# Seven products for both halves of the columns in seven K chunks, with their summed weights made in DRAM on a list of their own

## The chip, the cores and the metric

The kernel runs on one core of one Trainium2 chip. Such a core has a matrix engine (TensorE, in the profile PE, with its weight loads as PEld), a vector engine (VectorE, DVE), an engine for functions and copies (ScalarE, ACT), GpSimd (POOL) and SyncE (SP), each with an instruction queue that it works through in order. Matrix products read SBUF and write PSUM; 16 DMA engines move data between DRAM and SBUF, and within DRAM. SP, ACT and POOL issue DMAs from their queues. Engines wait for each other through semaphores.

The metric is the device time of one execution in microseconds. The kernel before takes 2182.21 us, the median of three runs (2182.13 to 2182.46).

## What is computed

Two layers work on x of 256 positions by 2048 features, in float32. Layer 0 has a mixer of pooling and attention, layer 1 an mLSTM mixer; each is followed by the same kind of feed-forward block, which this change is about:

```python
def conv_ffn(x, w_up, conv_w, conv_b, w_down):
    u = x @ w_up                                        # 2048 -> 2 * 5632
    up = jnp.pad(u, ((0, 0), (1, 1), (0, 0)))
    c = conv_w.astype(u.dtype)
    u = c[0] * up[:, :-2] + c[1] * up[:, 1:-1] + c[2] * up[:, 2:] + conv_b.astype(u.dtype)
    gate, val = jnp.split(u, 2, axis=-1)
    return (jax.nn.silu(gate) * val) @ w_down           # 5632 -> 2048
...
        x = x + conv_ffn(rms_norm(x, norm_ffn[layer]), w_up[layer], conv_w[layer], conv_b[layer], w_down[layer])
```

## The kernel before

**Numbers in two parts.** Each float32 operand is split into a high part (a rounded copy in the type float32r, made by ACT) and a low part (the rest, a subtraction on DVE). A product is then three products: high by high, high by low, low by high.

**Weights as a stream.** All weights come in one list of 128 x 1024 tiles (512 KB; some are half as wide), in the order in which TensorE needs them. `Stream` takes each through three steps: `load` (a DMA on SP into one of six raw buffers `w`), `split` (the ACT copy at L121 and the DVE subtraction at L122, into one of four buffers `hl`) and `next` (TensorE uses it). Loads are written out five tiles ahead of the use, splits two. Two kinds of entries are special. A `Sum` is loaded by `prepare` into a buffer `sum`: one DMA on SP, then a second one on POOL that adds onto it (L106, L107). A `Chain` is the tile behind a `Sum`: its own load on SP, and then two DVE additions of half a tile each (L117, L118), by which it becomes two further sums of weights. `Sum`s are prepared as soon as they stand within ten tiles of the use.

**The feed-forward block.** The 5632 inner features are worked on in six chunks of K, `FCH = [4, 8, 8, 8, 8, 8]` tiles of 128 features. An "up" unit (`up`, named `up` in the profile) computes one tile of 128 gate features and its 128 value features: 64 matmuls into one of two PSUM buffers `mm`, over four weight tiles. Behind it ACT and DVE gather the result, multiply it by the norm, do the convolution and the SiLU gate, and write the two parts of the inner activation `g`. Then chunk c's activation is multiplied by the down weights and added to x.

The down product of a chunk is done in two ways. The ordinary way (`down`, in the profile `dn`) multiplies by a block of 512 of the 2048 output columns. The other way is the scheme of seven products for a 2 by 2 block matrix product in the place of eight (a Strassen form with few additions): positions are halved (128 and 128), a pair of K tiles is the inner halves, and a half of the columns (1024) is the two blocks of 512. `combine` makes the sums of activations of one pair (`sf`, `s3`, `s1`), the host lays out sums of weights as far as two terms go, and `Sum` and `Chain` make the rest. Per pair there is an A step (four products, 12 matmuls, two weight tiles) and a B step (three products, 9 matmuls, one tile and a half one), named `pp` in the profile. Over the pairs of a chunk the products add up in PSUM (`ps`, four buffers), and at the last pair DVE adds them onto x and onto three running sums `acc` (`unit`). `total` adds the running sums to x, six additions, once all chunks are through.

Which half goes which way is said by `_halves`: in each of the first five chunks the second half (h = 1) goes by seven products and the first half by `down`; the last chunk is all ordinary (`down_two`, `down`, `down_end`). `BOTH`, chunks with seven products for both halves, is empty.

**What sets the order.** `_ffn_plan` writes the order of the block: chunk c's products are spread between the up units of chunk c + 1. Each up unit of a chunk of eight is followed by one step: A of pairs 0 to 3, then B of pairs 0 to 3; two of them also by an ordinary product. I call an up unit's followers a slot. TensorE's instructions run in exactly the written order. Those of the other engines are ordered by a list scheduler ahead of time, by its own timeline. Small tasks beside the main work (norms, attention heads, totals) are generators in `Weave`, which the code resumes at points of a clock of its own that each product advances (`tick`); an up unit counts 10.32 there, and four blocks of the output projection 82.6.

**Names and lines that the change touches.** `Stream.load` and `prepare` (L89 to L108), `Weave` (from L146), `mm` (L237), `combine` (L947), `unit` and `total` (from L968 and L1013), the loop over the plan (L1085), `_halves`, `_ffn_plan`, `_down_chunks`, `_ffn_weights` (from L1160). POOL's queue also holds the reciprocal square roots of all norms (L245); ACT's also the row copies for the mLSTM heads (L795).

Of the kernel before, what the change touches and what calls it, by code (L numbers as in the profile page):

```python
# [9 lines left out]
F32 = mybir.dt.float32  # L10
# [23 lines left out]
CH = 8  # L34
BOTH = ()
NEG = -1.0e30
# [34 lines left out]


class Chain:

# [5 lines left out]
class Stream:  # L80
# [8 lines left out]
    def load(self, pieces=1):  # L89
        i = self.n_load  # L90
        self.n_load += 1
        src = self.srcs[i]
        if isinstance(src, Sum):
            i in self.w or self.prepare(i)
            return
        src = src.src if isinstance(src, Chain) else src
        width = src.shape[-1]
        n = width // pieces
        w = self.wpool.tile([P, CH * P], F32, tag="w", name=f"w{i}")
        for c in range(0, width, n):  # L100
            self.nc.sync.dma_start(w[:, c : c + n], src[:, c : c + n])
        self.w[i] = w, n, width

    def prepare(self, i):
        w = self.sums.tile([P, CH * P], F32, tag="sum", name=f"sum{i}")
        self.nc.sync.dma_start(w, self.srcs[i].one)  # L106
        self.nc.gpsimd.dma_start(w, self.srcs[i].other, accum_op=ALU.add)  # L107
        self.w[i] = w, CH * P, CH * P  # L108
# [37 lines left out]
class Weave:  # L146


    def __init__(self):
        self.t, self.q = 0.0, []  # L150
# [40 lines left out]
@with_exitstack  # L191
def trunk(ctx: ExitStack, tc: tile.TileContext, gx, xT, xn, call, catt, cml, weights, out):
    nc = tc.nc
# [39 lines left out]
    def gain(n, k):  # L233
        c = n * KT + k
        return gcol[:, c : c + 1]

    def mm(out_, lhsT, rhs, start, stop):  # L237
        pe.matmul(out_, lhsT, rhs, start=start, stop=stop, skip_group_check=True)  # L238

# [462 lines left out]
    def mlstm_layer(norm, nxt):  # L702
        with ExitStack() as es:
# [203 lines left out]
    def ffn_layer(layer, norm, nxt):  # L907
        with ExitStack() as es:
# [59 lines left out]
            def unit(kind, c, h, j):  # L968
# [33 lines left out]
                else:  # L1002
# [4 lines left out]
                    if c == len(FCH) - 2:  # L1007
                        wv.add(total(h), 12.0 if h else 2.0)

# [74 lines left out]
            f, gts = 0, []  # L1084
            for kind, c, i, *j in _ffn_plan():  # L1085
                if kind == "up":
# [72 lines left out]

def _halves(c):  # L1160

    return () if c == len(FCH) - 1 else (0, 1) if c in BOTH else (1,)


def _ffn_plan():

# [5 lines left out]
    for c, n in enumerate(FCH):  # L1172
        pairs = FCH[c - 1] // 2 if c else 0
        units = [(kind, c - 1, h, j) for h in (_halves(c - 1) if c else ()) for kind in "AB" for j in range(pairs)]
        per = max(1, len(units) // n)

        busy = {u[3]: k // per for k, u in enumerate(units) if u[0] == "A"}
        for i in range(n):
            seq.append(("up", c, i))
            seq += units[i * per : i * per + per]  # L1180
            if len(_halves(c - 1)) == 1:
                for b in range(2):
                    if pairs and i == (b + 1) * pairs // 2 - 1:
                        seq.append(("down", c - 1, b))
# [5 lines left out]
def _down_chunks(w):  # L1190


    out, k0 = [], 0
    for c, n in enumerate(FCH):
        rows = w[k0 * P : (k0 + n) * P]
        blocks = [_mov(rows[:, b * 512 : b * 512 + 512]) for b in range(NB) if b // 2 not in _halves(c)]
        if c == len(FCH) - 1:
# [16 lines left out]

def _ffn_weights(up, parts):

    down = iter(parts[0])
    out, u = [], 0
    for kind, c, i, *j in _ffn_plan():
        if kind == "up":  # L1220
# [4 lines left out]
        elif kind != "mix":  # L1225
            s0, s1, r, ba, bb = parts[1 + 5 * i : 6 + 5 * i]
            q = sum(FCH[:c]) // 2 + j[0]
            out += [Sum(s0[q], s1[q]), Chain(r[q])] if kind == "A" else [ba[q], bb[q]]
    return out

# [99 lines left out]
```

## Time and profile before

| | |
|---|---|
| median of three runs | 2182.21 us |
| the profiled execution | 2182.76 us, of which the span of its instructions is 2181.0 us |
| granted TensorE clock | 1.0 |
| busy share: TensorE, DVE, ACT, POOL | 100%, 77%, 63%, 3% |
| weights and data moved by DMA | 462.95 MB |

In time, attention and its output projection end near 256 us; layer 0's feed-forward block runs to 980, the mLSTM mixer with its output projection to 1457, layer 1's feed-forward block to the end. The trace is read by groups (what a kind of instruction takes), by waits (who waited for whom), by the chain that ended last, by order of time, and by stretches (busy time of each engine between two points of time). Names are those of the program: `w` a raw weight tile, `hl` a split one, `xx` the normed x in two parts. A matmul's or a copy's duration includes its start and its end, which overlap with its neighbours; from start to start it is shorter.

### The profile page before, as it was taken

The numbers are of one execution on the slowest core, as the hardware profiler recorded it, in microseconds if no ns is written. First come the engines' busy times: TensorE is split into PE (matmuls) and PEld (weight loads), VectorE is DVE, ScalarE is ACT, GpSimd is POOL, SyncE is SP. The second block draws the span as 40 slices with busy tenths as digits, with TensorE's granted clock in tenths as the row PEclk, the third lists the DMA queues.
The fourth block names the chain that finished last, engine by engine and source line by source line (L and its number), as shares of the span: only waits on it lengthen the run. The fifth ranks groups of instructions, "written<-read, shape, count | busy, mean of one in ns | idle before, by whom it ended". The sixth has DMA issues, their size and how long they took to land.

```text
span 2181.0 us, 31219 instructions
## 1 busy us (share of the span) xinstructions
PE 2175.4 (100%) x11508; PEld 1862.8 (85%) x11508; DVE 1670.8 (77%) x2366; ACT 1370.6 (63%) x2166; POOL 59.3 (3%) x76
## 2 busy tenths in 40 slices
PE   9999999999999999999999999999999999999999
PEld 7888888888888888889888888888888888888887
DVE  7686688887878788776777676668888787878776
ACT  7665576766767576666454554557676666757663
POOL 0010000000000000000000000000000000000000
PEclk9999999999999999999999999999999999999999
DMA  9556567676877766656465555756768677776664
GB/s 326 178 169 203 174 199 235 206 244 206 256 226 245 229 221 215 219 193 205 160 201 182 180 179 175 223 182 197 232 205 243 214 240 236 242 230 227 215 213 163
DMA packets 133595, 462.95 MB, mean 212 GB/s; under 512 B 14810, under 2 KB 17154, under 8 KB 133442
## 3 DMA queue, kind: packets, MB, share of 16 engines
q1 hardware_dynamic: 125024, 438.08, 60.0%
q0 software_dynamic: 5344, 19.14, 5.2%
q10 hardware_dynamic: 3074, 3.75, 0.7%
q8 instruction: 90, 1.47, 0.3%
q14 instruction: 63, 0.52, 0.1%
HBM read 458.76 MB, written 2.14 MB: 211 GB/s over the span
## 4 chain that ended last, share of the span: by engine, by line
PE 99%; DMA 1%; DVE 0%; ACT 0%; issue 0%; SPq 0%; DVEq 0%
PE up L238 44%; PE dn L238 12%; PE op L238 8%; PE pp L238 8%; PE mv L238 4%; PE mq L238 4%; PE mk L238 4%; PE mo L238 4%; PE qproj L238 3%; PE pool L238 1%; PE vproj L238 1%; PE kproj L238 1%; PE qk L238 1%; PE av L238 1%; PE end L238 0%; PE xt L289 0%
## 5 line engine op out<-in xcount | busy, mean ns | idle before, releaser
L122 DVE TENSOR_TENSOR hl<-w,hl 128x1024 fp32r<-128x1024 f32 (+2 forms) x808 | 952.4, 1192 | 258.4 <-ACT hl L121 255.9
L121 ACT CAST hl<-w 128x1024 fp32r<-128x1024 f32 (+2 forms) x807 | 816.1, 1028 | 464.4 <-PE up L238 146.0
L238 PE MATMUL up<-xx,hl 128*128 128x512 f32 (+1 forms) x5632 | 993.9, 337 | 0.4 <-DVE hl L122 0.4
L238 PEld LDWEIGHTS up<-xx,hl 128*128 128x128 f32 x5632 | 866.9, 188 | 131.1 <-DVE hl L122 0.8
L238 PE MATMUL dn<-hl,g 128*128 128x512 f32 x1200 | 277.3, 390 | 0.0
L238 PEld LDWEIGHTS dn<-hl,g 128*128 128x128 f32 x1200 | 224.8, 188 | 46.7
L401 ACT COPY tb_up<-up 128x512 f32<-128x512 f32 x88 | 51.7, 587 | 133.3 <-PE up L238 133.3
L238 PE MATMUL pp<-hl,s 128*128 128x512 f32 x432 | 111.2, 393 | 0.0
L936 ACT ACTIVATE y<-tb_up,cst 128x256 f32<-128x256 f32 x176 | 103.8, 590 | 0.0
L402 DVE TENSOR_TENSOR tb_up<-up,tb_up 128x512 f32<-128x512 f32 x88 | 60.7, 690 | 56.0 <-ACT tb_up L401 55.7
L937 DVE TENSOR_TENSOR y<-y,z 128x510 f32<-128x510 f32 x88 | 60.5, 688 | 49.7 <-ACT y L936 49.7
L934 ACT ACTIVATE z<-tb_up,cst 128x256 f32<-128x256 f32 x176 | 88.5, 503 | 11.2 <-DVE tb_up L929 10.8
L238 PE MATMUL mk<-xx,hl 128*128 128x512 f32 (+1 forms) x512 | 92.1, 337 | 0.0
L238 PE MATMUL mq<-xx,hl 128*128 128x512 f32 (+1 forms) x512 | 92.1, 337 | 0.0
L238 PE MATMUL mv<-hl,xx 128*128 128x512 f32 (+2 forms) x480 | 91.7, 350 | 0.0
L238 PE MATMUL op<-hl,cat 128*128 128x512 f32 x384 | 91.6, 393 | 0.0
L238 PEld LDWEIGHTS pp<-hl,s 128*128 128x128 f32 x432 | 78.5, 188 | 15.1
L238 PE MATMUL mo<-hl,xx 128*128 128x512 f32 x384 | 90.5, 391 | 0.0
L238 PE MATMUL op<-hl,mcat 128*128 128x512 f32 x384 | 89.5, 392 | 0.0
L238 PEld LDWEIGHTS mq<-xx,hl 128*128 128x128 f32 x512 | 79.2, 188 | 11.6
L238 PEld LDWEIGHTS mk<-xx,hl 128*128 128x128 f32 x512 | 79.0, 188 | 11.4
L238 PEld LDWEIGHTS mv<-hl,xx 128*128 128x128 f32 x480 | 78.3, 189 | 11.2
(234 smaller groups left out, 1987.3 us busy)
## 6 DMA issues: line engine op xcount, KB each, us to landing
w<-in_up SPq DMA_DIRECT2D x352, 512.0 KB, 4.3
w<-in_dn SPq DMA_DIRECT2D x176, 512.0 KB, 4.7
w<-in_m_in SPq DMA_DIRECT2D x124, 512.0 KB, 4.1
w<-in_a_in SPq DMA_DIRECT2D x46, 512.0 KB, 4.4
sum<-in_dn SPq DMA_DIRECT2D x36, 512.0 KB, 4.8
sum<-in_dn POOLq DMA_DIRECT2D x36, 512.0 KB, 7.7
w<-in_a_out SPq DMA_DIRECT2D x32, 512.0 KB, 3.5
w<-in_m_out SPq DMA_DIRECT2D x32, 512.0 KB, 4.2
```

What stands on the lines that cost most here:

```text
L121: (self.nc.vector.tensor_copy if i + c == 0 else self.nc.scalar.copy)(hl[:, 0, c : c + n], w[:, c : c + n])
L122: self.nc.vector.tensor_sub(hl[:, 1, c : c + n], w[:, c : c + n], hl[:, 0, c : c + n].bitcast(F32))
L238: pe.matmul(out_, lhsT, rhs, start=start, stop=stop, skip_group_check=True)
L401: a.copy(tb, ps[:, :, 1, :])
L402: v.tensor_add(tb, ps[:, :, 0, :], tb)
L934: a.activation(z[:, 0, j, :], u[:, j, :], AF.Copy, scale=cw(tl, 0))
L936: a.activation(y[:, j, :], u[:, j, :], AF.Identity, scale=cw(tl, 1), bias=cw(tl, 3))
L937: v.tensor_add(y[:, :, 1:S], y[:, :, 1:S], z[:, 0, :, 0 : S - 1])
```

## The change

Seven chunks go over to seven products in both halves: chunks 2, 3 and 4 of layer 0, and 1 to 4 of layer 1. Their slots hold two steps each: A of pairs 0 and 1, A of 2 and 3, B of 0 and 1, B of 2 and 3 for the second half of the columns, then the same four for the first half. No ordinary product stands in these chunks. In the other chunks the slots stay as they were.

The first half's sums of weights are not made by `Sum` and `Chain`. `premix` makes them in DRAM: per pair, a scratch of two tiles, two plain copies issued on ACT's queue (one term into the first tile, one into the second), then, each on POOL's queue, an accumulation of the other term onto the first tile, one of the first tile onto a half of the second, and one of that half onto the other half. Between the steps lies a gap on the clock: 26 in layer 0 (started in the attention mixer), 28 in layer 1 (started in the mLSTM mixer); a new pair starts every 26 or 28, from the ninth on every 60 in layer 0. They stand on a list of their own (`side`), of which every due entry is resumed at each tick. Each of these DMAs waits for the matmul written out last before it (`paced`). The stream then loads the finished tiles as plain tiles (`Made`).

Beside that, the sums' buffers in SBUF go from two to three, the scratch `sf` moves into the buffer `sq` that the norms use for squares, and `total` starts after a delay of 2.0 (second half, in a chunk with both) or 10.0 in the place of 12.0 and 2.0.

```diff
-BOTH = ()
+BOTH = ((2, 3, 4), (1, 2, 3, 4))
...
+class Made:
+    ap = None
...
-        src = src.src if isinstance(src, Chain) else src
+        src = src.src if isinstance(src, Chain) else src.ap if isinstance(src, Made) else src
...
-        w = self.sums.tile([P, CH * P], F32, tag="sum", name=f"sum{i}")
+        w = self.sums.tile([P, CH * P], F32, tag="sum", bufs=3, name=f"sum{i}")
...
+    def aside(self, gen, delay):
+        self.side.append([self.t + delay, gen])
...
     def tick(self, dt):
         self.t += dt
+        for e in list(self.side):
+            while e in self.side and e[0] <= self.t:
+                try:
+                    e[0] = self.t + next(e[1])
+                except StopIteration:
+                    self.side.remove(e)
...
     def mm(out_, lhsT, rhs, start, stop):
-        pe.matmul(out_, lhsT, rhs, start=start, stop=stop, skip_group_check=True)
+        last_mm[0] = pe.matmul(out_, lhsT, rhs, start=start, stop=stop, skip_group_check=True)
...
+    scratch = pool("mixed", 1, space=bass.MemoryType.DRAM)
+    add = {"accum_op": ALU.add}
+    now = mybir.DependencyInfo(mybir.DependencyClass.Sync, mybir.DependencyReason.DATA)
+
+    def paced(ins):
+        tc.add_manual_dep(ins.ins, last_mm[0].ins.name, now, reason="paced")
+
+    def premix(layer, gap, late):
+        def one(i, s0, s1, r, made):
+            m = scratch.tile([P, 2, CH * P], F32, tag=f"m{layer}{i}", name=f"m{layer}_{i}")
+            h = CH * P // 2
+            steps = [(nc.scalar, m[:, 0], s0, {}), (nc.scalar, m[:, 1], r, {}), None,
+                     (g, m[:, 0], s1, add), None, (g, m[:, 1, :h], m[:, 0, :h], add), None,
+                     (g, m[:, 1, h:], m[:, 1, :h], add)]
+            for e in steps:
+                if e is None:
+                    yield gap
+                    continue
+                eng, to, src, kw = e
+                paced(eng.dma_start(to, src, **kw))
+            for j in range(2):
+                made[j].ap = m[:, j]
+
+        for i, e in enumerate(mixes[layer]):
+            wv.aside(one(i, *e), min(i + 1, 8) * gap + max(i - 7, 0) * late)
...
+            premix(0, 26.0, 60.0)
...
+            premix(1, 28.0, 28.0)
...
-                sf = t1p.tile([P, 4, P], F32, tag="sf", name=f"sf{layer}_{c}_{j}")
+                sf = sm1.tile([P, 512], F32, tag="sq", name=f"sf{layer}_{c}_{j}").rearrange("p (a b) -> p a b", a=4)
...
-                        wv.add(total(h), 12.0 if h else 2.0)
+                        wv.add(total(h), 2.0 if h and 0 in _halves(layer, c) else 10.0)
...
-        units = [(kind, c - 1, h, j) for h in (_halves(c - 1) if c else ()) for kind in "AB" for j in range(pairs)]
-        per = max(1, len(units) // n)
...
+        if halves == (0, 1):
+            slots = [units(kind, h, js) for h in (1, 0) for kind in "AB" for js in ((0, 1), (2, 3))]
+        else:
+            slots = [units(kind, 1, (j,)) for kind in "AB" for j in range(pairs)]
+            for b in range(2 if pairs else 0):
+                slots[(b + 1) * pairs // 2 - 1].append(("down", c - 1, b))
...
+            if kind == "B":
+                out += [ba, bb]
+            elif i:
+                out += [Sum(s0, s1), Chain(r)]
+            else:
+                made = [Made(), Made()]
+                mixes.append((s0, s1, r, made))
+                out += made
```

More of the change, by code (lines that the diff above doesn't have):

```diff
@@ L149, in __init__ @@
     def __init__(self):
-        self.t, self.q = 0.0, []
+        self.t, self.q, self.side = 0.0, [], []
         self.free = {"pr": 2, "pt": 2, "qt": 2}
@@ L191, in trunk @@
 @with_exitstack
-def trunk(ctx: ExitStack, tc: tile.TileContext, gx, xT, xn, call, catt, cml, weights, out):
+def trunk(ctx: ExitStack, tc: tile.TileContext, gx, xT, xn, call, catt, cml, weights, mixes, out):
     nc = tc.nc
@@ L235, in gain @@
         return gcol[:, c : c + 1]
+    last_mm = [None]
     def mm(out_, lhsT, rhs, start, stop):
-        pe.matmul(out_, lhsT, rhs, start=start, stop=stop, skip_group_check=True)
+        last_mm[0] = pe.matmul(out_, lhsT, rhs, start=start, stop=stop, skip_group_check=True)
     def rsqrt(ss, n, scale, name):
@@ L1084, in ffn_layer @@
             f, gts = 0, []
-            for kind, c, i, *j in _ffn_plan():
+            for kind, c, i, *j in _ffn_plan(layer):
                 if kind == "up":
@@ L1157, in _up_chunks, with _halves, _ffn_plan @@
     return np.ascontiguousarray(t.transpose(4, 0, 2, 1, 3, 5)).reshape(FT * (KT // 4), P, CH * P)
-def _halves(c):
-    return () if c == len(FCH) - 1 else (0, 1) if c in BOTH else (1,)
-def _ffn_plan():
+def _halves(layer, c):
+    return () if c in (-1, len(FCH) - 1) else (0, 1) if c in BOTH[layer] else (1,)
+def _ffn_plan(layer):
     seq = []
@@ L1173, in _ffn_plan, with units @@
         pairs = FCH[c - 1] // 2 if c else 0
-        units = [(kind, c - 1, h, j) for h in (_halves(c - 1) if c else ()) for kind in "AB" for j in range(pairs)]
-        per = max(1, len(units) // n)
-        busy = {u[3]: k // per for k, u in enumerate(units) if u[0] == "A"}
+        halves = _halves(layer, c - 1)
+        def units(kind, h, js):
+            return [(kind, c - 1, h, j) for j in js]
+        if halves == (0, 1):
[4 more added lines that the diff above has]
+                slots[(b + 1) * pairs // 2 - 1].append(("down", c - 1, b))
+        busy = {u[3]: k for k, slot in enumerate(slots) for u in slot if u[0] == "A"}
         for i in range(n):
             seq.append(("up", c, i))
[L1180 to L1184, printed above, removed]
+            seq += slots[i] if i < len(slots) else []
             if c < len(FCH) - 1:
@@ L1187, in _ffn_plan, with _down_chunks @@
     return seq + [("two", len(FCH) - 1, 0)] + [("down", len(FCH) - 1, b) for b in range(2, NB)]
-def _down_chunks(w):
+def _down_chunks(layer, w):
     out, k0 = [], 0
@@ L1195, in _down_chunks @@
         rows = w[k0 * P : (k0 + n) * P]
-        blocks = [_mov(rows[:, b * 512 : b * 512 + 512]) for b in range(NB) if b // 2 not in _halves(c)]
+        blocks = [_mov(rows[:, b * 512 : b * 512 + 512]) for b in range(NB) if b // 2 not in _halves(layer, c)]
         if c == len(FCH) - 1:
@@ L1212, in _down_chunks, with _ffn_weights @@
     return res
-def _ffn_weights(up, parts):
+def _ffn_weights(layer, up, parts):
     down = iter(parts[0])
-    out, u = [], 0
-    for kind, c, i, *j in _ffn_plan():
+    out, u, mixes = [], 0, []
+    for kind, c, i, *j in _ffn_plan(layer):
         if kind == "up":
@@ L1225, in _ffn_weights @@
         elif kind != "mix":
[L1226 to L1229, printed above, removed]
+            s0, s1, r, ba, bb = (e[sum(FCH[:c]) // 2 + j[0]] for e in parts[1 + 5 * i : 6 + 5 * i])
+            if kind == "B":
[6 more added lines that the diff above has]
+                out += made
+    return out, mixes
 def _constants():
@@ L1307 @@
         arrays[f"up{l}"] = _up_chunks(i["w_up"][l])
-        for j, part in enumerate(_down_chunks(i["w_down"][l])):
+        for j, part in enumerate(_down_chunks(l, i["w_down"][l])):
             arrays[f"dn{l}{j}"] = part
@@ L1319, in ffn @@
     def ffn(l):
-        return _ffn_weights(chunks(f"up{l}"), [chunks(f"dn{l}{j}") for j in range(11)])
+        out, m = _ffn_weights(l, chunks(f"up{l}"), [chunks(f"dn{l}{j}") for j in range(11)])
+        mixes.append(m)
+        return out
+    mixes = []
     n = 3 * (MD + 32)
@@ L1325 @@
     with tile.TileContext(nc, schedule_with_timeline_sim=True) as tc:
-        trunk(tc, t["gx"], t["xT"], t["xn"], t["call"], t["catt"], t["cml"], weights, o)
+        trunk(tc, t["gx"], t["xT"], t["xn"], t["call"], t["catt"], t["cml"], weights, mixes, o)
     r = _run(nc, [{f"in_{k}": val for k, val in arrays.items()}], core_ids=[0])
```

## The prediction

> **What bounds the kernel now.** I read the page first (shares, the chain that ended last), then the waits of TensorE, then the chain in order of time inside one chunk of layer 0, then groups and stretches for the engines behind it.
>
> ```profile
> span 2181.0 us, 31219 instructions
> PE 2175.4 (100%) x11508; PEld 1862.8 (85%) x11508; DVE 1670.8 (77%) x2366; ACT 1370.6 (63%) x2166; POOL 59.3 (3%) x76
> PE 99%; DMA 1%; DVE 0%; ACT 0%; issue 0%; SPq 0%; DVEq 0%
> ...
> PE up L238 <- DVE hl L122: 0.4, 1, 0.4
> ```
>
> The last row is from the waits: past the start, TensorE waited once, for 0.4 us. So a matmul that goes is worth its full time, and anything that makes TensorE wait is paid in full. The price of the matmuls, from the chain in order of time (start, us, what):
>
> ```profile
> 686.01 11.14 PE up L238 x64
> 697.15 2.77 PE pp L238 x12
> 699.92 10.88 PE dn L238 x48
> ...
> 760.63 2.06 PE pp L238 x9
> ```
>
> An up unit is 11.14 us. An A step of the seven products (12 matmuls) is 2.77, a B step (9) 2.06; 48 matmuls of the ordinary product take 10.88, so one is 0.2267 us.
>
> **The change, part by part.** *Fewer matmuls.* For the first half of the columns, layer 0 gets seven products in chunks 2, 3, 4 and layer 1 in 1 to 4: 7 chunks of 4 pairs, 28 pairs. A pair had 24 matmuls and gets 21: 84 fewer, 84 x 0.2267 = **19.0 us** off TensorE, all on the path. More cannot be gained, but for the 0.4 us wait.
>
> *More splitting.* A pair's ordinary weights are 2 tiles of 512 KB; the seven products need 3 and one half tile. DVE's rows, and its spacing when nothing holds it up:
>
> ```profile
> L122 DVE TENSOR_TENSOR hl<-w,hl 128x1024 fp32r<-128x1024 f32 x762 | 921.5, 1221 | 247.5 <-ACT hl L121 245.2
> L121 ACT CAST hl<-w 128x1024 fp32r<-128x1024 f32 x762 | 786.8, 1050 | 428.7 <-PE up L238 122.1 <-PE op L238 68.7 <-PE dn L238 67.6
> L122 DVE TENSOR_TENSOR hl<-w,hl 128x512 fp32r<-128x512 f32 x40 | 27.4, 686 | 8.3 <-ACT hl L121 8.1
> ...
> 738.90 1.22 DVE L122 TENSOR_TENSOR hl<-w,hl 128x1024 fp32r<-128x1024 f32 x1
> 740.04 0.68 DVE L997 TENSOR_TENSOR acc<-acc,pp 128x512 f32<-128x512 f32 x1
> 740.64 1.22 DVE L122 TENSOR_TENSOR hl<-w,hl 128x1024 fp32r<-128x1024 f32 x1
> ```
>
> From start to start a split holds DVE 1.14 us and a 512-wide add 0.60. A chunk gains 4 x (1.14 + 0.60) of splits and, at its end, 8 additions out of PSUM for 4 residual ones: 7.0 + 2.4 = 9.4 us. ACT gains 4 x (1.05 + 0.62) = 6.7. Before, a chunk's stretch holds:
>
> ```profile
> 580.00:710.00 130.00, 130.00 (x693) 111.45 (x692) 106.48 (x143) 87.60 (x136) 3.44 (x4) 1.00 0.75 234
> ```
>
> The columns after the length are busy time of TensorE, its weight loads, DVE, ACT and POOL, then clock, DMA share and GB/s. DVE goes from 106.5 of 130 us to 116 of 127.3, 82 to 91%; ACT from 67 to 74%. On the mean neither binds.
>
> *Where it is tight.* Split tiles live in four buffers, so a tile's cast waits until TensorE is through the fourth one before it. In the last stage:
>
> ```profile
> 2133.51 32.64 PE dn L238 x144
> 2166.14 10.89 PE end L238 x48
> ...
> 2163.46 1.05 ACT L121 CAST hl<-w 128x1024 fp32r<-128x1024 f32 x1 [1.67 <-PE dn L238]
> 2164.55 1.23 DVE L122 TENSOR_TENSOR hl<-w,hl 128x1024 fp32r<-128x1024 f32 x1 [1.49 <-ACT hl L121]
> ```
>
> A tile there lasts 12 matmuls, 2.72 us; one ended at 2166.14 - 2.72 = 2163.42, and the split that it released ended at 2165.78: **2.36 us** from release to split, if both engines are free. The change runs two pairs in a row after an up unit. In a B slot the tiles last 1.36, 0.68, 1.36, 0.68 us; the next up unit's first tile is released at 1.36 and due at 4.08, a lead of 2.72. That fits by 0.36, and by 0.45 more, since its first two matmuls use the high part alone. Walking DVE's order in the built program through each of the eight slots with the spacings above, most tiles arrive on time with 0 to 1 us to spare.
>
> One does not. From the start of a chunk's last B slot to the third tile of the up unit behind it, DVE has, when a chunk with chain additions follows: gather add, half split, multiplication by the norm, split, two additions out of PSUM, a chain addition, split, two more out of PSUM, two chain additions, a convolution addition, and that tile's split. With 0.65 us for ACT's copy ahead of the gather add, eleven at 0.60 and 1.14 + 1.14 + 1.22 for the splits this ends at 0.65 + 6.6 + 3.5 = 10.75. The tile's low part is due at 4.08 + 2 x 2.79 + 0.45 = 10.1. So TensorE waits 0.65 us. Five of the seven chunks are followed so (two in layer 0, three in layer 1): 5 x 0.65 = 3.3 us. The ends: nothing, as the before kernel shows no such wait, and twice that, 6.5, if the hand-overs between ACT and DVE cost as much again. Once late, TensorE gives the next slot that much slack.
>
> *Chain additions* (for the second half of the columns, as before) stand early in DVE's order, and block it:
>
> ```profile
> DVE w L117 <- DMA w<-in_dn: 40.2, 24, 3.4
> w<-in_dn SPq DMA_DIRECT2D x176, 512.0 KB, 4.7
> ```
>
> 24 of 36 wait for a load, 1.7 us each, behind which splits stand. In the first slot of a chunk I find the addition at 4.1 us after the slot's start and its load issued near -0.4 (when its buffer's split ends): landing at 4.3 with the median 4.7. Behind it is a split with no slack. Bounds: nothing, or the longest wait 3.4 less the 0.65 that the slot before gave, 2.75 x 7 = 19 us. The median's 0.2 is nearest: 7 x 0.2 = 1.4 us.
>
> *Sums in DRAM.* Each of 28 pairs adds two 512 KB copies on ACT's queue and accumulations of 512, 256 and 256 KB on POOL's, each held until TensorE reaches the last matmul written out, or (POOL) also until the step before has landed.
>
> ```profile
> L107 POOL DMA_DIRECT2D sum<-in_dn x36 | 31.0, 862 | 1169.5 <-DVE tb_up L402 285.2 <-DMA sum<-in_dn 279.7 <-DVE hl L122 178.7
> 1018.38 0.33 ACTq L795 DMA_DIRECT2D G<-gd  x1
> ACT hl L121 <- PE op L238: 68.7, 48, 1.8
> ```
>
> On POOL 84 x 0.86 = 72 us of issue over some 1,100 us, on an engine 3% busy; behind them stand the reciprocal roots, due long after. On ACT 56 x 0.33 = 18 us, and casts stand behind the wait. But ACT already waits for TensorE there (1.4 us at a time in the out projection), and its tiles are split 3 x 2.72 - 2.36 = 5.8 us before they are due: that covers the wait. I take 0; without that cover it is 28 x 1.4 = 39 us at most, a new wait as long as each now. SP gets 56 more loads at 0.33 us, idle otherwise.
>
> *DMA.* Before:
>
> ```profile
> GB/s 326 178 169 203 174 199 235 206 244 206 256 226 245 229 221 215 219 193 205 160 201 182 180 179 175 223 182 197 232 205 243 214 240 236 242 230 227 215 213 163
> ...
> q1 hardware_dynamic: 125024, 438.08, 60.0%
> q0 software_dynamic: 5344, 19.14, 5.2%
> ...
> 1370.00:1455.00 85.00, 85.00 (x392) 70.35 (x391) 54.72 (x59) 41.72 (x59) 1.78 (x2) 1.00 0.65 211
> 1455.00:1537.00 82.00, 82.00 (x457) 70.96 (x456) 64.15 (x94) 57.13 (x92) 2.46 (x3) 1.00 0.63 199
> 1537.00:1640.00 103.00, 103.00 (x574) 89.22 (x573) 85.62 (x121) 74.02 (x124) 1.71 (x2) 1.00 0.69 218
> ```
>
> A MB costs 0.600 x 2181 / 438.08 = 3.0 us of all engines on q1, and 5.9 on q0. A pair's sums are 1.05 MB of copies and 1.05 of accumulation: 9.3 us if DRAM to DRAM goes like these; 6.3 if all goes at q1's rate, 12.4 if all at q0's. In layer 1 a pair starts every 28 us of the kernel's own clock, 28 x 11.14/10.32 = 30.2 real (an up unit counts 10.32 on that clock): 0.31 (0.21 to 0.41) on 0.63 to 0.69 for some 170 us. That is 0.94 to 1.00, full but not over. The raw tiles have six buffers, so a load is issued 6 x 2.72 = 16.3 us before its own cast can start, less 2.4 for the split that frees the buffer and 4.7 to land: another 9 us of lateness are hidden. I take 0; without that cover up to 0.10 x 170 = 17 us.
>
> *The rest.* The first half's products end with six additions into x, due before the last ordinary products are added.
>
> ```profile
> 933.00:980.00 47.00, 47.00 (x223) 39.00 (x222) 38.52 (x54) 29.66 (x50) 0.00 (x0) 1.00 0.57 184
> ```
>
> There DVE is busy for 38.5 of 47 us; 6 x 0.60 = 3.6 more fit, and on the kernel's clock they are done 17.8 behind the last B step, the two products 20.6 behind it. 0; without that cover 3.6 in each layer. The scratch for differences moves into the squares' buffer, which only the norms use; the third sums buffer lets loads start earlier: 0.
>
> Sum against the profiled execution (2182.76 us; the median of the runs is 0.55 lower): 2182.8 - 19.0 + 3.3 + 1.4 = 2168.5, less 0.55: **2168 us**.
>
> **Rivals.** *Clean.* DVE and ACT find the gaps and nothing waits: 2163 to 2166, say 2164. For it: 91% is not full, and TensorE hardly waits now. Against: the 10.75 us before that tile.
>
> *Slower: the four buffers bind in every slot.* If ACT or DVE is in another instruction when a tile is released, its 0.6 to 1.2 us eat the 0.36 to 0.8 of spare: 56 slots x 0.45 = 25 us, 2188. It decides from 19/56 = 0.34 us a slot. Against: the before kernel's shortest leads, one B step and an up tile (2.06 + 2.79 = 4.85 us), cost nothing.
>
> *DMA runs short while layer 1's sums are made* (1370 to 1540). With DRAM to DRAM at the dear end the share is 1.04 to 1.10, up to 17 us short; less the hidden 9, on top of the forecast: 2176. For it: no trace here shows DRAM to DRAM. The Trainium skill, DMA: Bandwidth & Descriptors, section Specifications, puts a core's HBM limit near 358 GB/s. Counted by bytes read and written, a pair moves 5.2 MB, 174 GB/s on 211 to 218: by that rule some 7% short over 170 us, 12 us, so about 2180 if nothing of it is hidden. The trace neither bears this out nor denies it: its highest slice has 326 GB/s.
>
> **How the numbers follow.** Forecast (2166 to 2177) 0.50, clean 0.22, buffers bind 0.14, DMA short 0.12; 0.02 for what I don't see. A change within 0.2% (4.4 us) can't be told from none. Faster takes the first two and over half of the DMA case, 0.79; same 0.06; slower 0.15. The range goes from 2162.5 (19.0 and the 0.4 us gained) to 2181, which leaves out the buffers' case and the DMA's tail.
>
> **What will show it.** The pp rows in place of dn ones, and 84 fewer matmuls. TensorE waiting for DVE's hl 3 to 5 us in all, in the up unit behind a chunk's last B slot. DVE near 91% in those chunks. DMA share under 1.0 between 1370 and 1540, with no load ending a TensorE wait. Chain additions' waits for loads no longer than 40 us in sum. I am wrong if TensorE's waits reach 15 us, or appear outside the feed-forward chunks.

## The result, and the profile after

The changed kernel takes 2195.29 us (median of four runs, 2190.20 to 2196.44) against 2182.22 before: a ratio of 1.0055, 95% interval 1.0038 to 1.0073. It is 0.55% slower; the forecast was 2168 us, faster, with a range that ended at 2181. The profiled execution took 2196.44 us.

The page of the changed kernel, its lines that answer to those shown of before (span, engines, DMA queues, shares of the chain that ended last):

```profile
span 2194.6 us, 31669 instructions
PE 2168.1 (99%) x11424; PEld 1848.7 (84%) x11424; DVE 1730.6 (79%) x2456; ACT 1410.2 (64%) x2228; POOL 131.7 (6%) x160
q1 hardware_dynamic: 133088, 460.10, 61.2%
q0 software_dynamic: 17440, 48.51, 13.6%
q10 hardware_dynamic: 11138, 33.11, 4.8%
PE 86%; DMA 7%; DVE 6%; issue 1%; ACT 1%; DVEq 0%; POOLq 0%; ACTq 0%; SPq 0%
```

The 84 matmuls are gone (11508 to 11424). In their place DMA and DVE have entered the chain, 7% and 6% of the span, where before TensorE had 99%. The waits of the changed kernel (who waited for whom: us in total, times, longest):

```profile
DVE w L123 <- DMA w<-in_dn: 36.5, 14, 7.2
PE up L256 <- DVE hl L128: 17.5, 15, 4.9
DVE w L123 <- DMA sum<-in_dn: 8.0, 3, 3.0
PE pp L256 <- DVE hl L128: 3.3, 3, 2.7
PE op L256 <- DVE hl L128: 0.5, 1, 0.5
```

TensorE waits 21.3 us for split weights, against 0.4 before. DVE's chain additions (L123) wait for loads about as long in sum as before (36.5 + 8.0 = 44.5 us against 40.2), but in fewer and longer waits, up to 7.2 us against 3.4.

The span grew by 13.6 us although 19.0 us of matmuls went, so 32.6 us are new. To see where, I took for every matmul the time from its start to the next one's start, less the median of its kind (same tiles, same shape), and summed this by stage, for this trace and those of the experiments below (us; stages by the time of the trace):

| kernel | to 250 | 250-610 (layer 0, first chunks) | 610-980 (layer 0, rest) | 980-1640 (mLSTM, layer 1's start) | from 1640 (layer 1, rest) | sum |
|---|---|---|---|---|---|---|
| before | 4.7 | 0.0 | 1.0 | 2.9 | -0.6 | 8.1 |
| changed | 5.0 | 19.6 | 5.5 | 4.8 | 6.2 | 41.1 |
| no sums in DRAM (e1) | 4.6 | 2.3 | 4.4 | 3.3 | 9.6 | 24.2 |
| before, with the sums alone (e2) | 4.5 | 16.0 | -0.2 | 3.3 | -0.9 | 22.8 |
| chain additions in order (e3) | 4.4 | 3.3 | 8.4 | 5.2 | 14.3 | 35.6 |
| sums spread (e4) | 5.8 | 12.1 | 3.0 | 3.3 | 8.5 | 32.7 |
| additions two splits ahead (e5) | 4.7 | 0.9 | 1.8 | 4.5 | 1.3 | 13.2 |
| both (e6) | 5.7 | 4.7 | 1.6 | 3.0 | 1.5 | 16.6 |
| two ahead, no sums (e7) | 4.8 | 0.4 | 1.7 | 2.9 | 1.6 | 11.4 |

Differences between kernels carry the argument, not single entries: how finely the kinds are drawn shifts some columns by up to 3 us, the same in every kernel, and the differences by less than 1. The changed kernel loses 33.0 us more than the one before, and 19.6 of them between 250 and 610 us: for the most part before the first product of both halves is computed (chunk 2's, near 580). There the chain in order of time (start, us, what) reads:

```profile
266.75 21.61 PE up L256 x124
...
290.71 11.52 DMA w<-in_dn
...
302.33 0.70 DVE w L123
...
305.54 5.39 PE up L256 x30
...
318.46 10.65 DMA w<-in_dn
...
332.88 10.59 PE up L256 x46
```

and the changed kernel's timeline around the first of these two loads (start, duration, engine, line, operation; in brackets what ended the idle time before it):

```profile
280.71 1.15 ACTq L469 DMA_DIRECT2D m<-in_dn  x2
280.98 0.87 POOL L469 DMA_DIRECT2D m<-in_dn  x1 [20.96 <-PE up L256]
282.38 0.81 POOL L469 DMA_DIRECT2D m<-m  x1 [0.53 <-PE up L256]
283.77 0.81 POOL L469 DMA_DIRECT2D m<-m  x1 [0.58 <-PE up L256]
...
293.19 1.22 DVE L128 TENSOR_TENSOR hl<-w,hl 128x1024 fp32r<-128x1024 f32 x1
...
302.33 0.69 DVE L123 TENSOR_TENSOR w<-w,sum 128x512 f32<-128x512 f32 x1 [7.25 <-DMA w<-in_dn]
...
304.26 1.22 DVE L128 TENSOR_TENSOR hl<-w,hl 128x1024 fp32r<-128x1024 f32 x1
...
305.54 4.68 PE L256 MATMUL up<-xx,hl 128*128 128x256 f32 x26 [2.79 <-DVE hl L128]
```

Three things meet. First, the sums' transfers come in a bunch. Every pair moves one step per gap of 26, and the pairs start 26 apart, so the steps of four different pairs fall due at one moment: two copies and three accumulations, 2 MB, within 3.1 us. Second, a load issued behind them takes 11.5 us. The median times to landing of what was issued from 280 to 291 us, the changed kernel's and then the kernel's before:

```profile
w<-in_up SPq DMA_DIRECT2D x3, 512.0 KB, 12.4
m<-in_dn ACTq DMA_DIRECT2D x2, 512.0 KB, 13.5
w<-in_dn SPq DMA_DIRECT2D x1, 512.0 KB, 11.5
```

```profile
w<-in_up SPq DMA_DIRECT2D x3, 512.0 KB, 4.4
w<-in_dn SPq DMA_DIRECT2D x1, 512.0 KB, 4.2
```

Third, DVE's next instruction is the chain addition on that very load, and it is not that tile's turn yet: splits of earlier tiles, which TensorE needs sooner and whose loads are there, stand behind it. In DVE's order in this trace 4 to 6 splits stand between the first of a tile's two chain additions (L123, the one that waits) and that tile's own split, and 2 to 5 behind the second. DVE stops for 7.25 us, the split at 304.26 is late, TensorE idles 2.79 us; at the second load 4.92.

The Trainium skill, DMA: Bandwidth & Descriptors, section Queues, rings and completion order, says that each DMA engine takes turns between the queue rows that have work, packet by packet. By that rule, with three rows at work (SP's loads, ACT's copies, POOL's accumulations), a load would take some three times as long, 12.6 us for 4.2, an estimate; the 11.5 to 12.4 of the trace are near it, but do not show it to be the reason.

By the rates worked out further down (3.0 us a MB for the copies, 6.6 for the accumulations) the five transfers alone hold all engines for some 10 us, an estimate, and a load served behind them would land about as late. That loads are late behind a bunch is shown here; in which way the engines share their time is not.

### The profile page after: what moved, and what is told of

It is laid out like the page before. It is cut to its first block, busy times and chain, and to the rows that moved or that the text cites. A ratio compares the mean times of both kernels' runs of the same rounds, so it can differ in the third digit from the quotient of the medians.

```text
span 2194.6 us, 31669 instructions
## 1 busy us (share of the span) xinstructions
PE 2168.1 (99%) x11424; PEld 1848.7 (84%) x11424; DVE 1730.6 (79%) x2456; ACT 1410.2 (64%) x2228; POOL 131.7 (6%) x160
## 3 DMA queue, kind: packets, MB, share of 16 engines
q0 software_dynamic: 17440, 48.51, 13.6%
## 4 chain that ended last, share of the span: by engine, by line
PE 86%; DMA 7%; DVE 6%; issue 1%; ACT 1%; DVEq 0%; POOLq 0%; ACTq 0%; SPq 0%
PE up L256 39%; PE pp L256 11%; PE op L256 5%; PE dn L256 5%; PE mv L256 4%; PE mq L256 4%; PE mk L256 4%; PE mo L256 4%; PE qproj L256 3%; DVE hl L128 3%; DMA w<-in_dn 2%; DMA w<-in_m_out 2%; DMA sum<-in_dn 2%; PE kproj L256 1%; PE pool L256 1%
## 5 line engine op out<-in xcount | busy, mean ns | idle before, releaser
L128 DVE TENSOR_TENSOR hl<-w,hl 128x1024 fp32r<-128x1024 f32 (+2 forms) x864 | 1002.2, 1176 | 225.4 <-ACT hl L127 222.7
L127 ACT CAST hl<-w 128x1024 fp32r<-128x1024 f32 (+2 forms) x863 | 858.7, 1015 | 425.0 <-PE up L256 106.4
L256 PE MATMUL pp<-hl,s 128*128 128x512 f32 x768 | 198.1, 393 | 3.3 <-DVE hl L128 3.3
L256 PEld LDWEIGHTS pp<-hl,s 128*128 128x128 f32 x768 | 141.3, 188 | 33.3 <-DVE hl L128 4.8
L256 PE MATMUL pp<-hl,g 128*128 128x512 f32 x576 | 152.4, 391 | 0.0
L256 PEld LDWEIGHTS pp<-hl,g 128*128 128x128 f32 x576 | 105.5, 188 | 20.8
L256 PE MATMUL dn<-hl,g 128*128 128x512 f32 x528 | 122.7, 390 | 0.0
L256 PEld LDWEIGHTS dn<-hl,g 128*128 128x128 f32 x528 | 98.6, 188 | 20.4
```

Source lines behind the costliest of these rows:

```text
L127: (self.nc.vector.tensor_copy if i + c == 0 else self.nc.scalar.copy)(hl[:, 0, c : c + n], w[:, c : c + n])
L128: self.nc.vector.tensor_sub(hl[:, 1, c : c + n], w[:, c : c + n], hl[:, 0, c : c + n].bitcast(F32))
L256: last_mm[0] = pe.matmul(out_, lhsT, rhs, start=start, stop=stop, skip_group_check=True)
```

## The experiments

Eleven kernels were run, and all are here. "Theory 1" is the meeting of the three things above; "theory 2" the rival from the prediction, split buffers or DVE too slow in the slots with two pairs.

**The sums not made (e1).**

```diff
-            wv.aside(one(i, *e), min(i + 1, 8) * gap + max(i - 7, 0) * late)
+            e[3][0].ap, e[3][1].ap = e[0], e[2]
```

The first half's A steps read the raw tiles in place of the sums, so this kernel leaves out part of the computation.

> Left out: the sums in DRAM are not made; the A steps of the first half read the unsummed weight tiles in their place, so that matmuls, splits and loads stay and the 56 copies and 84 accumulations go. Theory 1 (the transfers of the sums come in bunches, a load issued then lands after 10 to 13 us in place of 4 to 5, and a chain addition that stands early in DVE's order holds the splits behind it until then): the waits of TensorE between 290 and 610 us and the half clock behind two of them go, 17 us; the five waits of 0.9 us behind a chunk's last B slot stay (4.6 us): 2168 to 2173 us. Theory 2 (the four split buffers, or DVE at 90%, in the slots with two pairs): the waits stay, 2188 to 2196 us.

2180.0 us (2175.5 to 2184.9), ratio 0.9989 (0.9980 to 0.9998). The sums cost 15 us, as theory 1 had it, and the loss between 250 and 610 falls from 19.6 to 2.3. But it is 7 us above theory 1's range. Five waits of 0.92 us behind a last B slot are there as expected; most of the rest are behind chain additions that stop for a load, now without any sums in DRAM, the longest for instance (timeline):

```profile
1892.87 0.69 DVE L123 TENSOR_TENSOR w<-w,sum 128x512 f32<-128x512 f32 x1 [3.81 <-DMA sum<-in_dn]
1893.48 1.22 DVE L128 TENSOR_TENSOR hl<-w,hl 128x1024 fp32r<-128x1024 f32 x1
...
1894.76 2.50 PE L256 MATMUL up<-xx,hl 128*128 128x256 f32 x7 [2.33 <-DVE hl L128]
```

The slots with two pairs use up tiles faster, so the addition reaches a load, here a sum that POOL is still accumulating, sooner after its issue.

**The sums alone (e2).** The plan of before, with the sums made as in the changed kernel and read by nobody:

```diff
-BOTH = ((2, 3, 4), (1, 2, 3, 4))
+BOTH = ((), ())
+MIXED = ((2, 3, 4), (1, 2, 3, 4))
...
+    mixes = [(*(parts[k][j] for k in (1, 2, 3)), [Made(), Made()]) for j in pairs]
```

> The sums are made in DRAM as in the changed kernel, at the same points of the program, but nothing reads them: the products are those of the kernel before (seven products for the second half alone). Theory 1: TensorE waits between 290 and 610 us as in the changed kernel, 13 us and 4 us of half clock, and little elsewhere: 2194 to 2202 us. Theory 2: no both-halves slots, no waits: 2182 to 2185 us.

2197.2 us (2195.4 to 2201.0), ratio 1.0070 (1.0055 to 1.0086), inside theory 1's range: 15 us for the sums by themselves. By matmul starts 16.0 us are lost between 250 and 610 and nothing elsewhere, though layer 1's sums are more. Theory 2 falls as the main cause: there are no slots with two pairs. The waits between 250 and 610 us in this run (its lines are one further down, L124 is the chain addition):

```profile
DVE w L124 <- DMA w<-in_dn: 31.1, 8, 8.1
PE up L257 <- DVE hl L129: 8.7, 3, 4.1
PE pp L257 <- DVE hl L129: 1.7, 1, 1.7
```

That late loads are harmless elsewhere shows in the out projection of layer 1. Issued from 1370 to 1457 us, in the changed kernel and in the one before:

```profile
w<-in_m_out SPq DMA_DIRECT2D x27, 512.0 KB, 12.0
```

```profile
w<-in_m_out SPq DMA_DIRECT2D x23, 512.0 KB, 4.2
```

The median load there is nearly three times as late, and TensorE waited 0.5 us for it (the op row above). There are no chain additions in that stage; casts alone wait for loads.

**Chain additions in order (e3).** Each pinned right ahead of its own tile's split:

```diff
-            self.nc.vector.tensor_add(w[:, :half], w[:, :half], self.sum[:, :half])
-            self.nc.vector.tensor_add(w[:, half:], w[:, half:], w[:, :half])
+            keep = self.tc.keep_in_program_order
+            keep(self.nc.vector.tensor_add(w[:, :half], w[:, :half], self.sum[:, :half]))
+            keep(self.nc.vector.tensor_add(w[:, half:], w[:, half:], w[:, :half]))
...
+    st.tc = tc
```

> The changed kernel with the two additions of a chain tile kept at their place of the program in DVE's order, right ahead of that tile's own split (4 to 6 splits of other tiles stand between them in the changed kernel). The sums in DRAM are made in the same bunches. Theory 1: loads land as late as before, but DVE does not stop for them ahead of splits that are due sooner; the waits of TensorE between 290 and 610 us go, those behind the last B slots (where chain additions stand in the way too) may: 2166 to 2179 us. Theory 3 (the DMA engines are short, whoever waits for them): the waits stay with casts in the place of chain additions: 2188 to 2196 us. Theory 2: 2188 to 2196 us.

2193.7 us (2192.0 to 2194.9), ratio 1.0054 (1.0037 to 1.0071): no theory's range but the rivals'. By stages it is two results. Between 250 and 610 us the loss falls from 19.6 to 3.3 and no chain addition waits for a load any more, with the same bunches: theory 1. From 1640 on it grows from 6.2 to 14.3. The new waits stand in the first slot with two pairs of each chunk, 1.4 and 1.0 us in most (timeline; L124 and L125 are the additions, L128 and L129 the split's two halves):

```profile
1761.67 0.68 DVE L125 TENSOR_TENSOR w<-w 128x512 f32<-128x512 f32 x1
...
1762.43 3.89 ACT L128 CAST hl<-w 128x1024 fp32r<-128x1024 f32 x4 [2.90 <-issue]
...
1763.53 0.50 PE L258 MATMUL pp<-hl,s 128*128 128x512 f32 x1 [1.22 <-ACT hl L128]
...
1764.79 0.74 PE L258 MATMUL pp<-hl,s 128*128 128x512 f32 x2 [0.76 <-DVE hl L129]
```

ACT's cast of a chain tile needs both additions, and with a tile every 1.36 us in that slot there is no time for them ahead of the cast. So there is a worst place at either end: too early they wait for loads, too late the split waits for them.

**The sums spread (e4).** Each transfer of a pair a fifth of the gap behind the one before it, so that no two start together:

```diff
-            steps = [(nc.scalar, m[:, 0], s0, {}), (nc.scalar, m[:, 1], r, {}), None,
+            steps = [(nc.scalar, m[:, 0], s0, {}), None, (nc.scalar, m[:, 1], r, {}), None,
...
-                    yield gap
+                    yield gap / 5
```

> The changed kernel with the five transfers of a pair a fifth of the gap apart (about 5.5 us), so that no two of them start together; bytes, queues and the first transfer of each pair are as in the changed kernel. Theory 1: loads between 250 and 610 us land within 9 us, the waits of TensorE there fall from 13 us to under 5, and the half clock goes: 2178 to 2186 us. If it is the mean load of the DMA engines and not the bunches: no change, 2190 to 2196 us. Theory 2: 2190 to 2196 us.

2188.9 us (2187.3 to 2192.7), ratio 1.0032 (1.0019 to 1.0045), 6.4 us better than the changed kernel but above theory 1's range; the loss between 250 and 610 falls from 19.6 to 12.1, and the longest load issued from 250 to 336 us takes 7.5 us in place of 12.9. The bunching is less than half of what the sums cost there; single transfers of the sums still draw some loads out to 7 to 10 us, and an addition that comes some 4 us after its load's issue waits for those too.

**Additions two splits ahead (e5).** What e3 leaves to try is the middle: both additions written two splits ahead of their own and kept in program order.

```diff
+    def chain(self, i):
...
+        keep(self.nc.vector.tensor_add(w[:, :half], w[:, :half], s[:, :half]))
+        keep(self.nc.vector.tensor_add(w[:, half:], w[:, half:], w[:, :half]))
...
     def split(self, then=None):
         i = self.n_split
+        for j in range(3):
+            self.chain(i + j)
         w, n, width = self.w.pop(i)
...
```

> The changed kernel with the two additions of a chain tile pinned in DVE's order exactly two splits ahead of that tile's own split (in the changed kernel 4 to 6 ahead, in the kernel with them in order 0). Sums in DRAM in the same bunches. Theory 1, refined (4 to 6 ahead the addition comes some 4 us after its load's issue and DVE stops for a late load; 0 ahead the cast behind it is late in the slots with two pairs, 1.4 and 1.0 us in each of seven chunks): two ahead both kinds go. Left of the 33 us that the changed kernel lost beyond the kernel before are 3 to 13: 2166 to 2176 us. Rival (DVE at 90% in the slots with two pairs is late whatever the order): 10 us of waits in those chunks stay, 2180 to 2190 us. Rival (the late loads of the sums' bunches reach TensorE by the casts instead): 2185 to 2195 us.

**2168.3 us** (2167.1 to 2169.0), ratio 0.9934 (0.9918 to 0.9951), inside theory 1's range, 27 us better than the changed kernel and 14 better than the one before, with every transfer and every split still there. In the trace the first addition, the one that waits for loads, stands two splits ahead in all 36 tiles; the second does not stay there, it is two ahead in 13, one in 14 and none in 9. At the place shown above, the landing of the load issued from 280 to 291 us, and the timeline (L122, L123 are the additions here, L135 the split):

```profile
w<-in_dn SPq DMA_DIRECT2D x1, 512.0 KB, 11.5
```

```profile
297.17 2.35 DVE L135 TENSOR_TENSOR hl<-w,hl 128x1024 fp32r<-128x1024 f32 x2
300.35 1.23 DVE L135 TENSOR_TENSOR hl<-w,hl 128x1024 fp32r<-128x1024 f32 x1 [0.49 <-ACT hl L134]
302.02 0.69 DVE L122 TENSOR_TENSOR w<-w,sum 128x512 f32<-128x512 f32 x1 [0.44 <-DMA w<-in_dn]
```

The load still takes 11.5 us, but three more splits are done before DVE asks for it, and it waits 0.44 us in place of 7.25. A stretch with both halves (columns as in the prediction):

```profile
580.00:710.00 130.00, 129.62 (x689) 110.20 (x688) 115.28 (x156) 94.56 (x149) 5.80 (x7) 1.00 0.85 269
```

DVE is busy 115.3 of 130 us, and TensorE lacks 0.4. Theory 2 is out: DVE at 89% and four split buffers are fast enough.

**Both edits (e6).** The diffs of e4 and e5 together.

> Both edits at once: chain additions two splits ahead, and the transfers of the sums a fifth of the gap apart. Theory 1: if two ahead covers the bunches' loads, spreading adds nothing measurable, within 3 us of the kernel with two ahead alone; if not, it is better by what the loads still cost there: 2164 to 2174 us.

2171.9 us (2170.6 to 2173.0), ratio 0.9952 (0.9937 to 0.9967). This is 3.6 us slower than e5, just beyond the 3 us that I had allowed: once the additions stand right, spreading makes it worse. One place shows it, near 572 us, where a cast and an addition waited for a sum of the second half that was itself accumulating late (2.3 us of TensorE); why the spread hits it was not tested.

**Two ahead, no sums (e7).** The diffs of e1 and e5.

> Left out: the sums in DRAM are not made, the A steps of the first half read the unsummed tiles; chain additions two splits ahead. What is left above 2182.2 - 19.0 = 2163.2 us is then neither the sums' transfers nor the early additions. Theory 1: 2163 to 2168 us. Rival (DVE and the four split buffers are late in the slots with two pairs): 2172 to 2180 us, as in the kernel without sums and with early additions (2180.0).

2167.4 us (2167.1 to 2167.5), ratio 0.9931 (0.9917 to 0.9946), inside theory 1's range. So with the additions in the right place the sums in DRAM cost 0.9 us, against 15 with them early. Read the other way, moving the additions is worth 12.6 us without the sums (2180.0 to 2167.4) and 27.0 with them: not quite half of the price of the early additions has nothing to do with the sums.

**The kernel before with its additions two ahead (e8).** The same edit in the kernel before.

> The kernel before with its chain additions two splits ahead (4 to 6 ahead in it). TensorE waited for 0.4 us there, so theory 1 expects no difference: 2181 to 2183 us. If the place of the additions is worth something of its own, whatever the sums in DRAM: 2176 to 2180 us.

2182.1 us, ratio 0.9998 (0.9988 to 1.0007): in the kernel before, the place of the additions was worth nothing. Loads that land after 4 us are not the whole reason: in e1 the down tiles land after 4.4 us in the median (4.7 before), and there the move is worth 12.6 us. What e1 has and the kernel before has not are, above all, the slots with two pairs.

**One layer at a time (e9, e10).** `BOTH = ((2, 3, 4), ())` and `BOTH = ((), (1, 2, 3, 4))`, additions early as in the changed kernel.

> The change in layer 0 alone (chunks 2, 3, 4 there, 36 fewer matmuls, 12 pairs of sums in DRAM); layer 1 as in the kernel before; chain additions early, as the scheduler puts them. By the losses that the changed kernel's trace shows stage by stage, layer 0 lost 24 us between 250 and 980 us, against 36 x 0.2267 = 8.2 gained: theory 1 expects 2195 to 2200 us. If the slots with two pairs were what costs, a layer would cost by its chunks, 3 of 7 of the 32 us less 8.2: 2186 to 2190 us.

> The change in layer 1 alone (chunks 1 to 4 there, 48 fewer matmuls, 16 pairs of sums, most of them made while no chain additions run). The changed kernel's trace shows 8 us lost in its stages against 48 x 0.2267 = 10.9 gained: theory 1 expects 2177 to 2182 us. By chunks, 4 of 7 of 32 us less 10.9: 2187 to 2192 us.

Layer 0 alone: 2197.7 us, ratio 1.0071 (1.0056 to 1.0086), inside theory 1's range. Layer 1 alone: 2182.9 us, ratio 1.0003 (0.9993 to 1.0012), 0.9 above it; its 10.9 us of matmuls are just given back. It is layer 0, with fewer matmuls to win, that makes the change slower.

**One chunk more (e11).** Two ahead, and chunk 1 of layer 0 for both halves too (`BOTH = ((1, 2, 3, 4), (1, 2, 3, 4))`, gap of the late pairs 50 in place of 60).

> Chain additions two splits ahead, and chunk 1 of layer 0 with seven products for both halves as well (12 more matmuls gone, 4 more pairs of sums in DRAM, the late pairs 50 apart in place of 60). If the matmuls are the price and the rest is covered: 2168.3 - 2.7 = 2165 to 2167 us. If layer 0's sums begin to cost once more: 2168 to 2175 us.

2181.2 us (2178.5 to 2183.9), ratio 0.9996 (0.9986 to 1.0005): 13 us worse than e5, and beyond the range that I gave to the sums' costing again. Of the 27.7 us lost by matmul starts 17.4 lie between 250 and 980. Between 590 and 780 us, where sums of layer 0 are now still being made beside slots with two pairs, casts wait for loads:

```profile
ACT hl L134 <- DMA w<-in_up: 8.4, 6, 3.4
...
PE up L264 <- ACT hl L134: 3.5, 3, 1.9
```

The longest of these loads take 13.4 us, and DVE's additions waited there only once, for 1.2 us. So it is the cover of the casts that ends here, not that of the additions, and a kernel one chunk beyond e5 has lost e5's gain. Whether earlier sums would save this chunk was not tried.

## Why the prediction was wrong

*Fewer matmuls* (19.0 us): right in size. 84 are gone, and e5 and e7, where little else is left, sit at 2168.3 and 2167.4 against 2182.2 - 19.0 = 2163.2. That e5 comes out at the 2168 of the forecast is chance: it is another kernel, without the 3.3 us of waits that the sum held.

*More splitting* (neither engine binds on the mean): right, shown by e5's stretch: DVE 115.3 of 130 (116 of 127.3 forecast), ACT 94.6, TensorE 129.6.

*Where it is tight* (one tile late by 0.65 us in five chunks): right in place, number of times and mechanism. All five are in the changed kernel's trace at 695, 826, 1764, 1893 and 2024 us, each 0.92 us by the matmuls' starts, 4.6 in sum for 3.3. The instructions that I listed ahead of that split are the ones on DVE there, two chain additions among them:

```profile
692.31 0.68 DVE L1054 TENSOR_TENSOR x<-x,pp 128x512 f32<-128x512 f32 x1
692.91 0.68 DVE L123 TENSOR_TENSOR w<-w,sum 128x512 f32<-128x512 f32 x1
693.51 0.68 DVE L124 TENSOR_TENSOR w<-w 128x512 f32<-128x512 f32 x1
694.11 0.68 DVE L986 TENSOR_TENSOR y<-y,z 128x510 f32<-128x510 f32 x1
694.72 2.35 DVE L128 TENSOR_TENSOR hl<-w,hl 128x1024 fp32r<-128x1024 f32 x2
```

With the additions moved (e5) TensorE does not wait there at all; five waits of 0.33 us are new, each in the second A step behind that up unit.

*Chain additions* (1.4 us, 0 to 19): **this is the step that failed, together with the next but one.** I had found the addition 4.5 us after its load's issue, with the load landing at 4.7, so with no cover at all, and priced it with the median landing time of the kernel before. Without any sums it was mis-sized already: in e1 waits over 0.25 us other than the five and one at the start come to 7.8 us by the table's measure. And the median did not hold where it counted: loads issued behind a bunch of the sums' transfers landed after 11.5 us and more. The right sum was not (additions at before's loads) plus (loads at before's additions) but the one at the other's price. The term of 1.4 us is 27 us of the result, which is what moving the additions gave back: 12.6 of them in the slots with two pairs alone (4.6 at the five tiles above, 7.8 at the others), the other 14 only together with the sums in DRAM.

*Sums in DRAM, issue and held waits* (0): right. POOL and ACT issue them as costed, and e7 to e5 is 0.9 us for everything about the sums.

*DMA* (0, up to 17 without cover): **failed in its place and in its cover.** The volume was right: from e1 to the changed kernel, q0 gains 29.4 MB and 13.6% of 2194.6 less 4.8% of 2178.5 us, 194 us, 6.6 us a MB; q10 gains 29.4 MB and 88 us, 3.0 a MB; a pair is 10.1 us for 9.3 forecast. But I looked only at layer 1's 170 us (share 0.63 to 0.69), and not at layer 0's sums between 250 and 610, where the DMA share before was no lower and 19.6 us were lost:

```profile
250.00:610.00 360.00, 360.00 (x1948) 309.80 (x1947) 291.43 (x402) 246.54 (x391) 9.32 (x11) 1.00 0.70 222
```

Besides, I spread a pair's 9.3 us evenly over 30, where the transfers of four pairs start within 3 us; and I took the 9 us by which a load may be late for its own cast as the cover of every load. For casts it holds in the out projection, where loads of 12 us cost half a microsecond. A chain addition has none of it.

*The rest* (0): right as far as any run shows; the total's additions and the moved scratch end no wait of TensorE in any trace read here.

Of the rivals, "DMA runs short while layer 1's sums are made" came nearest to the cause, late loads, but by the mean share and in the wrong stage: in 1370 to 1540 TensorE lost about 1 us more than before, at a share of 0.92. "The four buffers bind in every slot" is the nearest in time (2188) and wrong: e5 and e7 have the same buffers and slots. None of the rivals forecast 2195. From 1370 to 1457 the changed kernel moved 276 GB/s with every byte counted once. Counted as in the prediction, with each read and write of the sums, that is some 370, an estimate: queues q0 and q10 moved 75 there against 12 before, and 63 times 1.5 comes on top. TensorE lost next to nothing there, so a limit on the mean rate was not what counted. By the Trainium skill, DMA: Bandwidth & Descriptors, section Specifications, near 358 GB/s would be the limit; no run here shows it, and the estimate lies above it.

Of the signs I had named, TensorE's waits "reach 15 us": they reached 21.3. "Chain additions' waits no longer than 40 us in sum" was a poor sign: 44.5 is hardly more than the 40.2 before. What changed is the length of single waits, up to 7.2 us, and behind that one TensorE stood still for 2.79 us.

## What to carry to other kernels

An instruction that stands early in an in-order engine's queue has only the cover from its own operand's issue to its own turn, however late its result is due; when a change adds DMA work anywhere, price every such wait with the landing times under the new load, in each stage where the new transfers run, and look at when they start, not only at their mean. If the trace shows an engine stopped for a load with ready work behind it, move that instruction back first: here two to four splits later for the first of two additions turned 0.55% slower into 0.66% faster, with nothing else changed. Do not move it as far back as it goes: with both additions right ahead of their own split (e3) the split was too late for the slots with two pairs.

## What the runs showed of the hardware

A wait of TensorE can cost more than its length. After the 4.9 us wait at 328 the granted clock fell to half (stretches of the changed kernel; columns as before):

```profile
328.00:330.00 2.00, 0.00 (x0) 0.00 (x0) 0.80 (x2) 0.00 (x0) 0.00 (x0) 1.00 1.07 305
...
332.00:334.00 2.00, 1.12 (x4) 1.02 (x5) 2.00 (x3) 2.00 (x3) 0.00 (x0) 0.50 0.26 45
334.00:336.00 2.00, 2.00 (x8) 1.71 (x7) 2.00 (x4) 0.50 (x2) 0.00 (x0) 0.50 0.74 268
```

Eight matmuls start in 2 us; an up unit at the full clock has 64 in 11.14, 11 to 12 in 2 us. The 46 matmuls from 332.88 took 10.59 us where 46/64 of an up unit are 8.0: 2.6 us on top of the wait; a second such stretch, behind the 2.7 us wait at 474, added about 1.5 (64 matmuls of an up unit in 12.59 us). I had priced waits at their length alone.

By the clock record of the trace the two stretches begin at 331.37 and 478.14 and last 6.83 and 3.41 us. They lie 146.77 us apart, 43 times 3.413. On a grid with that step the 3.4 us before the first stretch were idle throughout, of the 3.4 us before the second 2.3 were idle, and the wait of 2.8 us at 302, which no half clock followed, is cut at 304.07 into 1.3 and 1.5.

The Trainium skill, TensorE: Matmul & The Clock Gate, section Part 1: The HAM clock gate, puts the fall to half behind an idle window of about 3.4 us that runs freely. The stretches agree with it in length and in lying on one grid; they do not need the whole window to be idle: in this trace 2.3 us of it were enough, and 1.5 were not.
